# 130 constant matrix products of 26 forms ahead of the first real product of a two-layer encoder kernel

## The chip, the cores and the metric

The kernel runs on one core of a Trainium2 chip. The metric is the device time of one execution in microseconds. Two timed executions of the kernel before took 1747.62 and 1748.41 us; their median is 1748.01 us. A further execution was taken with the profiler, and every row quoted below is of that one; its span, from the first to the last instruction, is 1746.7 us.

The engines are named as the profile names them: PE is the matrix engine, PEld its loading of weights (which can run beside a product), DVE the vector engine, ACT the activation engine, POOL the general engine, SP the engine that issues most transfers. A product takes a block of weights of 128 rows and up to 128 columns, and a moving operand of 128 rows and up to 512 columns, and writes into one of eight banks of PSUM, the accumulation memory. All other tiles lie in SBUF, the on-chip memory, 128 partitions wide.

## The reference

Two layers of a speech encoder on 512 tokens of width 1024, in float32:

```python
for l in range(DEPTH):                                  # 2
    x = x + 0.5 * swiglu(rms_norm(x, ffn1_norm[l]), ffn1_w_gate[l], ffn1_w_up[l], ffn1_w_down[l])
    h = rms_norm(x, mix_norm[l])
    p = h @ w_in[l]
    attn = mla_group(p[..., :o_kv], p[..., o_kv:o_pe], p[..., o_pe:o_cv], ...)
    conv = conv_group(p[..., o_cv:], conv_w[l], conv_b[l], conv_ln_g[l], conv_ln_b[l])
    x = x + jnp.concatenate([attn, conv], axis=-1) @ w_out[l]
    x = x + 0.5 * swiglu(rms_norm(x, ffn2_norm[l]), ffn2_w_gate[l], ffn2_w_up[l], ffn2_w_down[l])
    x = rms_norm(x, post_norm[l])
```

`swiglu(x, g, u, d)` is `(silu(x @ g) * (x @ u)) @ d`, with an inner width of 2816. `mla_group` is chunk-causal attention with 8 heads on low-rank projections, `conv_group` a gated causal convolution of 31 taps with a layer norm.

## The kernel before

Everything is held with features on the partitions and the 512 tokens along the tile. To reach float32 accuracy, both operands of a large product are split into a high and a low part of type float32r, and each product of 128 features is three products on PE, in `mm3`: high by high (L209), high by low (L210), low by high (L211). Weights come from memory as float32 into tiles `raw` or `fr`, ACT copies out the high part (L157 in `load_w`, L299 in `split_into`), and DVE subtracts to get the low part (L164, L301). Both parts lie in one long tile, `weights`, used as a ring of four places for each part; a place can be filled again only when PE has used it. In most of the feed-forward work the moving operand has 256 columns (`HS`), elsewhere 512 (`S`).

Tiles for split activations and other passing data come from a pool named `ring` with 35 buffers (`slot()`, shown as `r` in the profile); each holds 512 float32, 2 KB in a partition. Banks of PSUM come from `bank()`, of which there are seven (`ps`).

The program is unrolled. Its text gives the order of priority; within that, and within the edges written by hand (`issue_after`, `in_turn`), a planner sets each engine's order of instructions and the places of the tiles by its own simulation of the program (`schedule_with_timeline_sim=True`). On the chip each engine then works through its list in order and waits on semaphores.

The opening, which the change touches, runs as follows. The first transfers are issued: one 4 KB row of gains by ACT (L129), the first piece of x by SP (L130). DVE fills `ones` with 1.0 (L133). PE then does ten float32 products of `ones` by `ones` into a bank that nobody reads (`awake`, L135 to L137; `WAKE` is 10); a float32 product is recorded as two passes, so there are 20 records. DVE fills further constants (L139 to L147). Meanwhile the pieces of x land, ACT and DVE split each into two parts (L222, L223), and ACT and DVE split the first weights, in halves of 512 columns (L1143, L1144). The first real products, each 512 columns wide, start as soon as the first piece of x and the first half of weights are there (L209 to L211, called from `plain_first`). While they go on, the sums of squares for the first norm are gathered (L239 to L246), and PE forms the norm's sums between the products of the first feed-forward block (L253); from these comes R, which scales every operand that follows (L389 and on).

Of the kernel before, what the change touches and what calls it, by code (L numbers as in the profile page):

```python
# [7 lines left out]
FP = mybir.dt.float32  # L8
FR = mybir.dt.float32r
BF = mybir.dt.bfloat16  # L10
# [5 lines left out]
P = 128  # L16
D = 1024
S = 512
# [19 lines left out]
HS = S // 2  # L38
# [45 lines left out]
def encoder_kernel(ctx: ExitStack, tc: tile.TileContext, xT, consts, vecs, rgain, wgu1, wd1, wdq1, wdr1,  # L84
# [11 lines left out]
    def nm(s):  # L96
        uid[0] += 1
        return f"{s}{uid[0]}"

    def slot(dt=FP, w=S):  # L100
        return ring.tile([P, w], dt, tag="r", name=nm("r"))
# [4 lines left out]
    def bank():  # L106
        return psum.tile([P, S], FP, tag="ps", name=nm("ps"))
# [14 lines left out]
    V, A, G, T = nc.vector, nc.scalar, nc.gpsimd, nc.tensor  # L122
# [12 lines left out]
    awake = bank()  # L135
    for _ in range(WAKE):
        T.matmul(awake[:, 0:P], ones, ones, start=True, stop=True)  # L137
    minus_half = cpool.tile([P, H], FP, name="minus_half")
    V.memset(minus_half, -0.5)  # L139
    onesm = cpool.tile([P, P], FP, name="onesm")  # L140
# [1191 lines left out]
```

## Time and profile before

| | before |
|---|---|
| median of two timed runs | 1748.01 us |
| the runs | 1747.62 to 1748.41 us |
| span of the profiled execution | 1746.7 us |
| PE busy | 1728.1 us, 12486 products |
| DVE busy | 1471.0 us |
| ACT busy | 1097.3 us |
| POOL busy | 388.7 us |
| moved by DMA | 231.56 MB, 133 GB/s on average |

Times in a row are starts from the beginning of the span, then durations. A row of the timeline may merge several instructions that follow each other (`x2`), and ends with the idle time before it and what ended that. The duration that the profile gives a product is its whole passage through the array, and products overlap: how fast they follow each other is read from their starts or from a count over a stretch, not from their durations. A record of a product is missing here and there.

### The profile page before, as it was taken

How to read it: one execution, taken by the hardware profiler on the slowest of the kernel's cores; microseconds unless marked ns; L12 is line 12 of the kernel's file. 1: busy time of each engine (PE TensorE's matmuls, PEld its weight loads, DVE VectorE, ACT ScalarE, POOL GpSimd, SP SyncE). 2: the span in 40 equal slices, each digit the busy share in tenths (PEclk: the TensorE clock that was granted, in tenths of full speed). 3: DMA queues.
4: the chain of work that ended last, by engine and by line, in shares of the span. 5: the costliest groups of instructions: out<-in, count | busy, mean ns of one | idle time of the engine just before them, and what ended most of it. 6: DMA issues, size and time to landing. Idle time of an engine off the chain costs nothing. (4 is left out here: it accounts for less than half of the span.)

```text
span 1746.7 us, 31482 instructions
## 1 busy us (share of the span) xinstructions
PE 1728.1 (99%) x12486; PEld 1579.1 (90%) x12486; DVE 1471.0 (84%) x2104; ACT 1097.3 (63%) x1711; POOL 388.7 (22%) x322
## 2 busy tenths in 40 slices
PE   9999999999999999999999999999999999999998
PEld 7899999888678899999889999997976788999997
DVE  7888888888965989897679989888989668888887
ACT  5576766567953476756645757665778435767665
POOL 1001000348823001000310010013676410010000
PEclk9999999999999999999999999999999999999999
DMA  5567575424303467675425575754251125675753
GB/s 184 144 155 185 142 197 112 136 88 118 80 25 102 116 160 177 159 172 138 124 72 163 131 202 133 196 121 130 83 148 35 56 83 145 155 184 143 191 117 101
DMA packets 76851, 231.56 MB, mean 133 GB/s; under 512 B 8736, under 2 KB 12960, under 8 KB 76704
## 3 DMA queue, kind: packets, MB, share of 16 engines
q1 hardware_dynamic: 58704, 171.87, 30.8%
q0 software_dynamic: 17856, 57.68, 19.3%
q8 instruction: 98, 1.61, 0.4%
q14 instruction: 49, 0.40, 0.1%
q10 hardware_dynamic: 144, 0.00, 0.0%
HBM read 225.33 MB, written 2.10 MB: 130 GB/s over the span
## 5 line engine op out<-in xcount | busy, mean ns | idle before, releaser
L210 PE MATMUL ps<-r,weights 128*128 128x256 f32 (+1 forms) x2620 | 810.2, 309 | 2.8 <-DVE r L223 2.8
L209 PE MATMUL ps<-r,weights 128*128 128x256 f32 (+1 forms) x2620 | 807.3, 311 | 0.8 <-ACT weights L1143 0.6
L211 PE MATMUL ps<-r,weights 128*128 128x256 f32 (+1 forms) x2380 | 741.2, 313 | 5.9 <-DVE weights L301 3.9
L210 PEld LDWEIGHTS ps<-r,weights 128*128 128x128 f32 x2620 | 492.0, 188 | 35.3 <-DVE r L223 4.1
L209 PEld LDWEIGHTS ps<-r,weights 128*128 128x128 f32 x2620 | 491.9, 188 | 33.9 <-issue 2.0
L211 PEld LDWEIGHTS ps<-r,weights 128*128 128x128 f32 x2380 | 446.8, 188 | 38.9 <-DVE weights L301 5.4
L209 PE MATMUL ps<-xj,weights 128*128 128x256 f32 x864 | 238.5, 276 | 0.0
L210 PE MATMUL ps<-xj,weights 128*128 128x256 f32 x864 | 238.5, 276 | 0.0
L299 ACT CAST weights<-fr 128x1024 fp32r<-128x1024 f32 (+2 forms) x178 | 168.4, 946 | 96.2 <-DVE fr L453 40.1
L157 ACT CAST weights<-raw 128x1024 fp32r<-128x1024 f32 (+4 forms) x124 | 112.1, 917 | 177.7 <-PE ps L210 114.0
L301 DVE TENSOR_TENSOR weights<-fr,weights 128x1024 fp32r<-128x1024 f32 (+2 forms) x178 | 195.1, 1096 | 31.4 <-ACT weights L299 31.3
L433 POOL DMA_DIRECT2D ls<-in_wgu x72 | 62.5, 868 | 703.1 <-ACT ls L432 619.9
L164 DVE TENSOR_TENSOR weights<-raw,weights 128x1024 fp32r<-128x1024 f32 (+4 forms) x108 | 119.8, 1118 | 64.1 <-ACT weights L157 63.4
L210 PEld LDWEIGHTS ps<-xj,weights 128*128 128x128 f32 x864 | 162.2, 188 | 0.0
L209 PEld LDWEIGHTS ps<-xj,weights 128*128 128x128 f32 x864 | 162.2, 188 | 0.0
L211 PE MATMUL ps<-xj,ls 128*128 128x256 f32 x576 | 159.0, 276 | 0.0
L301 DVE TENSOR_TENSOR weights<-raw,weights 128x1024 fp32r<-128x1024 f32 (+2 forms) x112 | 122.0, 1089 | 14.1 <-ACT weights L299 13.9
L299 ACT CAST weights<-raw 128x1024 fp32r<-128x1024 f32 (+2 forms) x112 | 105.2, 939 | 42.9 <-DVE raw L532 23.5
L1005 POOL TENSOR_TENSOR y<-y,pr 128x495 f32<-128x495 f32 (+29 forms) x90 | 119.3, 1328 | 45.8 <-ACT pr L1003 40.5
L432 ACT ACTIVATE ls<-fr 128x1024 fp32r<-128x1024 f32 (+2 forms) x62 | 59.9, 967 | 97.9 <-PE ps L211 64.2
L516 DVE SCALAR_TENSOR_TENSOR x<-ps,x 128x512 f32<-128x512 f32 x154 | 105.7, 686 | 8.6 <-PE ps L211 7.9
L211 PEld LDWEIGHTS ps<-xj,ls 128*128 128x128 f32 x576 | 108.1, 188 | 0.0
(260 smaller groups left out, 3013.9 us busy)
## 6 DMA issues: line engine op xcount, KB each, us to landing
fr<-in_wgu SPq DMA_DIRECT2D x112, 512.0 KB, 4.6
ls<-in_wgu POOLq DMA_DIRECT2D x72, 512.0 KB, 7.2
raw<-in_wgu SPq DMA_DIRECT2D x62, 512.0 KB, 5.3
fr<-in_wdq SPq DMA_DIRECT2D x48, 384.0 KB, 4.4
ls<-in_wdq POOLq DMA_DIRECT2D x32, 384.0 KB, 6.4
raw<-in_wd SPq DMA_DIRECT2D x32, 256.0 KB, 2.8
raw<-in_wcv SPq DMA_DIRECT2D x16, 512.0 KB, 3.5
raw<-in_wout SPq DMA_DIRECT2D x16, 512.0 KB, 3.4
```

Source lines behind the costliest of these rows:

```text
L157: order["cast"] = in_turn("h", lambda: A.copy(hi[:, :w], raw[:, :w]))
L164: in_turn(e, lambda: e.tensor_tensor(lo[:, :w], raw[:, :w], hi[:, :w].bitcast(FP), ALU.subtract))
L209: T.matmul(o, lh, rh, start=first, stop=False, skip_group_check=free)
L210: T.matmul(o, lh, rl, start=False, stop=False, skip_group_check=free)
L211: order["mm"] = T.matmul(o, ll, rh, start=False, stop=last, skip_group_check=free).ins
L299: in_turn("h", lambda: A.copy(hi[:, :w], src[:, :w]))
L301: order["lo"] = in_turn(V, lambda: V.tensor_tensor(lo[:, :w], src[:, :w], hi[:, :w].bitcast(FP), ALU.subtract))
L432: A.activation(lo[:, :n], src[:, :n], AF.Copy, scale=-1.0)
L433: G.dma_start(out=lo[:, :n], in_=w, accum_op=ALU.add)
L516: return V.scalar_tensor_tensor(v, o.rearrange("p (m t) -> p m t", m=2), 0.5 * sign, v, ALU.mult, ALU.add).ins
L1005: order["conv"] = G.tensor_tensor(ys[c][:, s:], ys[c][:, s:], pr[:, s:], ALU.add).ins
```

## The change

Directly behind the ten products of `ones` in the program's text, three slots of the ring are taken and filled by DVE: `pm` and `pw` of type float32r, 512 columns each, and `pb` of type bfloat16, 512 columns. Then PE does 26 groups of five equal products into the bank `awake`, 130 products in all. Nothing reads their result. The five of a group have the same weights and the same moving operand; the groups differ in these:

- 8 groups with 512 moving columns and 8 with 256, in which the weights start 0, 16, ... 112 elements into `pw`;
- 4 groups with 256 moving columns, weights starting 4, 8, 24 and 192 elements into `pw`;
- 256 moving columns that are all one column of `pm`, read with step zero; and 128 weights that are all one column of `pw`, with 256 moving columns;
- bfloat16 weights and moving operand, 256 and 512 columns;
- weights of 64 columns, with 256 and with 512 moving columns.

```diff
     awake = bank()
     for _ in range(WAKE):
         T.matmul(awake[:, 0:P], ones, ones, start=True, stop=True)
+    pm, pw = slot(FR), slot(FR)
+    pb = slot(BF)
+    V.memset(pm.bitcast(FP), 1.0)
+    V.memset(pw.bitcast(FP), 1.0)
+    V.memset(pb, 1.0)
+    forms = [(pw[:, 16 * j:16 * j + P], pm[:, 0:n]) for n in (S, HS) for j in range(8)]
+    forms += [(pw[:, j:j + P], pm[:, 0:HS]) for j in (4, 8, 24, 192)]
+    forms += [(pw[:, 0:P], pm[:, 0:1].to_broadcast([P, HS])), (pw[:, 16:17].to_broadcast([P, P]), pm[:, 0:HS]),
+              (pb[:, 0:P], pb[:, 0:HS]), (pb[:, 0:P], pb[:, 0:S]), (pw[:, 0:64], pm[:, 0:HS]), (pw[:, 0:64], pm)]
+    for w_, m_ in forms:
+        for _ in range(5):
+            T.matmul(awake[0:w_.shape[1], 0:m_.shape[1]], w_, m_, start=True, stop=True)
     minus_half = cpool.tile([P, H], FP, name="minus_half")
     V.memset(minus_half, -0.5)
```

## The prediction

> **What bounds the kernel now.** I read the page first: its span, the busy times and the costliest groups.
>
> ```profile
> span 1746.7 us, 31482 instructions
> ...
> PE 1728.1 (99%) x12486; PEld 1579.1 (90%) x12486; DVE 1471.0 (84%) x2104; ACT 1097.3 (63%) x1711; POOL 388.7 (22%) x322
> ...
> L210 PEld LDWEIGHTS ps<-r,weights 128*128 128x128 f32 x2620 | 492.0, 188 | 35.3 <-DVE r L223 4.1
> ```
>
> PE is busy for 99% of the span, so only 18.6 us of 1746.7 are without a product. A share of busy time alone would not show that PE is at its pace, so I read second the table by stretches.
>
> ```profile
> 30.00:50.00 20.00, 20.00 (x88) 16.23 (x87) 19.70 (x31) 8.94 (x15) 0.00 (x0) 1.00 0.22 65
> 50.00:100.00 50.00, 48.99 (x322) 43.84 (x322) 42.70 (x60) 30.04 (x43) 3.67 (x4) 1.00 0.60 159
> ...
> 300.00:400.00 100.00, 97.34 (x593) 87.60 (x592) 88.17 (x127) 60.68 (x113) 42.87 (x33) 1.00 0.36 102
> 400.00:500.00 100.00, 98.72 (x664) 71.53 (x663) 89.82 (x176) 74.30 (x160) 66.75 (x50) 1.00 0.31 84
> ...
> 1300.00:1400.00 100.00, 99.29 (x649) 70.39 (x648) 78.74 (x131) 69.78 (x150) 56.76 (x40) 1.00 0.22 62
> ...
> 1600.00:1700.00 100.00, 100.00 (x883) 99.92 (x883) 88.48 (x120) 66.43 (x93) 9.52 (x11) 1.00 0.63 155
> ```
>
> The columns after the length are busy time and count of PE, PEld, DVE, ACT and POOL, then PE's granted clock, the share of the DMA engines and GB/s. The last row is the feed-forward work at its pace: 883 products of 256 columns in 100 us, 113.3 ns each, at granted clock 1.00. A weight load takes 188 ns there (the row above) and still a product starts every 113 ns, so loads run beside products. DVE is busy for 88% of it and DMA for 63%: neither sets the pace. PE does, and work added to PE's list is paid for unless it falls where PE waits.
>
> So the third view is the timeline of the opening, where the change lies: PE's rows from the last products of `ones` on.
>
> ```profile
> 4.21 1.05 PE L137 MATMUL ps<-ones 128*128 128x128 f32 x6
> 5.07 0.50 PE L209 MATMUL ps<-r,weights 128*128 128x512 f32 x1
> 5.41 0.44 PE L210 MATMUL ps<-r,weights 128*128 128x512 f32 x1
> 6.46 0.50 PE L209 MATMUL ps<-r,weights 128*128 128x512 f32 x1 [0.60 <-ACT weights L1143]
> 6.79 0.40 PE L210 MATMUL ps<-r,weights 128*128 128x512 f32 x1
> 7.03 0.66 PE L211 MATMUL ps<-r,weights 128*128 128x512 f32 x2
> 7.54 0.72 PE L209 MATMUL ps<-r,weights 128*128 128x512 f32 x2
> 8.32 0.50 PE L210 MATMUL ps<-r,weights 128*128 128x512 f32 x1
> 8.66 0.40 PE L211 MATMUL ps<-r,weights 128*128 128x512 f32 x1
> 8.90 0.39 PE L210 MATMUL ps<-r,weights 128*128 128x512 f32 x1
> 9.13 0.40 PE L211 MATMUL ps<-r,weights 128*128 128x512 f32 x1
> 9.36 0.62 PE L209 MATMUL ps<-r,weights 128*128 128x512 f32 x2
> 9.82 0.39 PE L210 MATMUL ps<-r,weights 128*128 128x512 f32 x1
> ```
>
> The first real product starts at 5.07 us, right behind the products of `ones`. Until about 9.4 us the starts are uneven, because data arrives late; from then on they are even. The pace of 512 columns comes from the groups in the stretch 10 to 24.7 us and its last row of L210:
>
> ```profile
> L210 PE MATMUL ps<-r,weights 128*128 128x512 f32 x23 | 8.9, 389 | 0.0
> L211 PE MATMUL ps<-r,weights 128*128 128x512 f32 x22 | 8.2, 389 | 0.0
> L209 PE MATMUL ps<-r,weights 128*128 128x512 f32 x21 | 7.4, 389 | 0.0
> ...
> 24.55 0.39 PE L210 MATMUL ps<-r,weights 128*128 128x512 f32 x1
> ```
>
> These are 66 products, the first the one at 9.82 (it reaches past 10), the last the one at 24.55: 65 steps in 14.73 us, 226.6 ns each, twice the 113.3 ns of 256 columns.
>
> **The change, part by part.** *The products.* 512 columns move in 8 groups of the first kind, one of bfloat16 and one with 64 weight columns: 10 groups, 50 products. 256 columns move in 8 + 4 + 2 (the two broadcasts) + 1 + 1 = 16 groups, 80 products. By the paces above: 50 x 0.2266 + 80 x 0.1133 = 11.33 + 9.06 = 20.4 us. All are ahead of the real products in the program, and no operand of theirs comes from a transfer, so I put them on PE from 5.07 us to 25.5 us without a gap.
>
> The trace shows no bfloat16 product of this size, no broadcast operand, and no weights at these offsets under one moving tile. From above, the nearest row is a float32 product at L272, two passes of 512 columns; from below, products of 32 weight columns at L705, which share the array in strips:
>
> ```profile
> 30.81 1.02 PE L272 MATMUL ps<-t,ones 128*128 128x512 f32 x2
> ...
> 31.89 0.40 PE L210 MATMUL ps<-r,weights 128*128 128x512 f32 x1
> ...
> 445.96 3.60 PE L705 MATMUL ps<-r,m 128*32 128x512 f32 x32
> ```
>
> The two passes of L272 and one product of L209 lie between 30.81 and 31.89: (1.08 - 0.23) / 2 = 0.425 us a pass, 1.9 times 0.2266. If every form went at that, the products would cost 38.3 us. L705 does 32 products in 3.60 us, 0.113 us each, half of 0.2266; if the bfloat16 and the 64-column forms (20 products, 3.4 us of the sum) went at that, the sum would be 18.7 us. I take 20.4, because 110 of the 130 are float32r products of full weights, which is what L209 to L211 are.
>
> Here the Trainium skill has a lower price: the page "TensorE: Matmul & The Clock Gate", section "Back-to-back issue gap", states N / 2.4 + 2.5 ns, 215.8 ns for 512 columns and 109.2 for 256, by which the sum would be 19.5 us and the time 0.9 us lower. The trace has 226.6 and 113.3 at granted clock 1.00, so it does not agree, and the measured paces are used.
>
> *The fills.* DVE gets three fills of 512 elements ahead of its other constants.
>
> ```profile
> 0.84 0.17 DVE L133 MEMSET ones<- 128x128 f32 x1 [0.84 <-PEq L1324]
> ...
> 1.38 0.11 DVE L147 MEMSET mneg<- 1x64 bf16 x1
> 4.54 0.75 DVE L223 SCALAR_TENSOR_TENSOR r<-x,first_gain,r 128x512 fp32r<-128x512 f32 x1 [3.05 <-ACT r L222]
> ```
>
> 128 float32 take 0.17 us, so 512 take at most four times that, 0.68; three fills take at most 2.0 us. DVE is then done with its constants at about 3.5 us, and its next work starts at 4.54 after 3.05 us of idling. I cost the fills at nothing; if that idling were gone they would delay the first split by up to 2.0 us, which again would lie under the new products. `pm` and `pw` are filled by about 2.4 us, long before PE is through with `ones` at 5.07. No transfer is added, and SP's, ACT's and POOL's lists are untouched.
>
> *The stalls that go.* From 5.07 to 9.82 PE started 14 products (the rows above), which at the even pace need 14 x 0.2266 = 3.17 us; 4.75 passed. With the first real product at 25.5 us those 1.58 us of waiting should go, since what they waited for is done by then:
>
> ```profile
> 9.56 1.35 DVE L1144 TENSOR_TENSOR weights<-raw,weights 128x512 fp32r<-128x512 f32 x2
> 10.99 2.79 DVE L223 SCALAR_TENSOR_TENSOR r<-x,first_gain,r 128x512 fp32r<-128x512 f32 x4
> ```
>
> The first weights are split by 10.91 us and all of x by 13.78. Nothing is late next up to the norm's sums, because PE had no gap from 9.4 to 25.7 us before.
>
> *Later waits.* ACT, DVE and SP get 18.8 us ahead of PE in the opening, but cannot keep it: the four places of the `weights` ring come free only by PE, and R comes from PE's sums. After R, DVE is the late one (19.70 of 20 us busy in the row 30 to 50), and PE's next wait ends on it:
>
> ```profile
> 65.91 0.50 PE L211 MATMUL ps<-r,weights 128*128 128x512 f32 x1 [0.91 <-DVE weights L164]
> ```
>
> That work cannot start before R, so I let this wait stand and move with the rest (if it went, 0.9 us less). The three slots leave 32 of 35 in the ring until 25.5 us; the opening needs 16 for x and one for the squares, so no tile waits for them. They are free again when the operands after R are made.
>
> *Sum.* +20.4 - 1.6 = +18.8 us. The span of the profiled execution would be 1746.7 + 18.8 = 1765.5 us. The median of the timed runs stands 1.3 us above that span, and from it the time is 1748.0 + 18.8 = 1766.8 us, 1.1% more.
>
> **The rivals.** *A load is not hidden behind a product that uses the same weights.* This is the one that would make it slower by over 2%. Each group repeats one block of weights, and the stream of the trace changes blocks at nearly every product. If a load of 188 ns stood ahead of each new product, the sum would be 20.4 + 130 x 0.188 = 44.8 us and the time 1748.0 + 44.8 - 1.6 = 1791.2 us. It decides from a mean cost of 281 ns a product on, since 2% is 35.0 us and 35.0 + 1.6 over 130 is 0.281 (I have 0.157). For it: nothing in the trace repeats float32r weights. Against it: the products of `ones` do repeat theirs, and their loads run beside them,
>
> ```profile
> 4.22 0.85 PEld L137 LDWEIGHTS ps<-ones 128*128 128x128 f32 x5
> ```
>
> five loads in 0.85 us, less than 5 x 0.188, and the products in step with them. I give it 3 in 100. The Trainium skill has a sentence on its side: the page "TensorE: Matmul & The Clock Gate", section "The mechanism", has loads overlap products in flight only when their row groups differ, and here all 128 rows are used by each. The trace speaks against it: 188 ns loads over all 128 rows under products 113.3 ns apart.
>
> *Some offsets clash.* Weights and moving operand are both read from SBUF, and a bad distance might slow a read. If the 100 products of the 20 offset groups (40 x 0.2266 + 60 x 0.1133 = 15.9 us of the sum) took from a tenth to nine tenths more (the latter being L272's pace), the time would be 1768 to 1781 us. Against it: the same 113.3 ns holds over 100 us in which tiles from all over the ring meet weights at many places. For it: the weights there start at few distinct offsets. I give 9 in 100 to a clash that adds more than 2 us.
>
> *The planner orders the rest anew.* With 20 us more on PE its simulation may place tiles and order instructions differently far behind the opening. What it can win or lose is PE's waiting in the stretches that depend on order: 1.0 + 2.7 + 1.3 + 0.7 = 5.7 us in the rows 50 to 100, 300 to 500 and 1300 to 1400 above. All of it gone, or doubled, gives 1761 to 1772.5 us. Against it: most edges around the products are written out by hand. I give a shift of more than 2 us 13 in 100.
>
> *The products cost nothing.* That the time does not grow needs PE to have 18.8 us of later waits to give; outside the opening the whole span has less than 18.6. One in 100, the same for a planner's gain beyond that.
>
> **How the numbers follow.** The main case, 74 in 100, is 1766.8 us, by itself 1765 to 1769 (from 18.7 us of products to 2 us more than the sum). With the planner's ends and the lower half of the clash the range is 1761 to 1775; outside it I leave the upper clash, the unhidden loads and the no-cost case, about one in 10. The measurement tells about 2%, 35 us, from no change. Slower by over 2%: the unhidden loads and nothing else, 0.03. Faster by over 2%: no case gives it; 0.01 for what I do not see. Within 2%: 0.96.
>
> **What would show it.** In the profile after: 130 more products ahead of the first L209; the bfloat16 groups apart from the others in pace; the first L209 near 25.5 us, with even starts from there; PE busy near 1748 us; the wait that ends on L164 still there, 19 us later. A first L209 after 28 us means a clash or unhidden loads, to be read from the starts within each group. A first L209 near 25.5 us with a span outside 1764 to 1768 means that something behind the opening was reordered.

## The result and the profile after

The changed kernel took 1767.93 and 1769.65 us in two runs, a median of 1768.79 us against 1748.01 us: a ratio of 1.0113, 95% interval 1.0097 to 1.0130, or 20.8 us more (17 to 23 us by the interval). That is within the forecast range of 1761 to 1775 us and 2.0 us above the forecast of 1766.8 us. Against the 2% that was set as the measure, it counts as no change. The span of the profiled execution grew from 1746.7 to 1766.2 us, by 19.5 us. The trace after is that of the execution timed at 1767.93 us, 1.7 us above its span. The span before stands as far below the timed 1748.41 us, so that trace is most likely of this timed execution and not of a further one; the medians differ by more than the spans because the other two executions lie further apart.

The page of the kernel after, its first lines (busy time, share of the span and count of each engine):

```profile
span 1766.2 us, 31747 instructions
...
PE 1749.2 (99%) x12615; PEld 1598.6 (91%) x12616; DVE 1472.5 (83%) x2107; ACT 1099.1 (62%) x1711; POOL 388.3 (22%) x322
```

PE has 129 records more (one of the 130 is missing) and is busy for 21.1 us more; the other engines are busy as before. The timeline of PE in the opening of the kernel after, in rows that merge equal products; lines of the code are 12 higher behind the insertion, so that L221 is the old L209:

```profile
1.06 4.64 PE L137 MATMUL ps<-ones 128*128 128x128 f32 x20 [1.06 <-DVE ones L133]
5.35 18.25 PE L149 MATMUL ps<-r,r 128*128 128x512 f32 x110
23.44 1.80 PE L149 MATMUL ps<-r 128*128 128x256 bf16 x9
24.89 2.08 PE L149 MATMUL ps<-r,r 128*64 128x256 f32 x10
26.81 0.39 PE L221 MATMUL ps<-r,weights 128*128 128x512 f32 x1
27.04 0.40 PE L222 MATMUL ps<-r,weights 128*128 128x512 f32 x1
...
85.89 0.50 PE L223 MATMUL ps<-r,weights 128*128 128x512 f32 x1 [0.91 <-DVE weights L176]
```

The products stand where they were put, without a gap, and the first real product starts at 26.81 us instead of 5.07. From there the starts are even, 0.23 us apart: the stalls of the old opening are gone. The wait on the low part of the weights (old L164, now L176) is still there and as long as before, 0.91 us, at 85.89 instead of 65.91 us.

Setting each real product of one trace beside the same product of the other shows where the 20 us lie. It can be done for all, since both have 12486 records of products outside the new line, in nearly the same order:

```
start before, us        5.07    6.46    9.36   58.42    96.2 to 1536   1549 to 1707   1740.71 (last)
later by, us           21.74   20.81   20.18   20.09   19.9 to 20.3           19.4             20.01
```

All of it comes in the opening. In the following 1480 us it stays between 19.9 and 20.3 us. At 1549 us one wait of the trace before is not in the one after; the run with the fills alone, below, lacks it too, so it is not the products that took it away.

### The profile page after: what moved, and what is told of

It is laid out like the page before. It is cut to its first block, busy times and chain, and to the rows that moved or that the text cites. A ratio compares the mean times of both kernels' runs of the same rounds, so it can differ in the third digit from the quotient of the medians.

```text
span 1766.2 us, 31747 instructions
## 1 busy us (share of the span) xinstructions
PE 1749.2 (99%) x12615; PEld 1598.6 (91%) x12616; DVE 1472.5 (83%) x2107; ACT 1099.1 (62%) x1711; POOL 388.3 (22%) x322
## 4 chain that ended last, share of the span: by engine, by line
PE 68%; DVE 7%; ACT 2%; issue 1%; DMA 1%; SPq 0%; DVEq 0%; ACTq 0%
PE ps L223 21%; PE ps L221 21%; PE ps L222 21%; DVE cv L1011 1%; DVE mx L919 1%; PE ps L960 1%; PE ps L938 1%; DVE x L528 0%; ACT weights L311 0%; DVE x L646 0%; PE ps L717 0%; DVE r L941 0%; DVE weights L176 0%; DMA r<-m 0%; PE ps L265 0%
## 5 line engine op out<-in xcount | busy, mean ns | idle before, releaser
L221 PE MATMUL ps<-r,weights 128*128 128x256 f32 (+1 forms) x2620 | 808.0, 311 | 0.1
L221 PEld LDWEIGHTS ps<-r,weights 128*128 128x128 f32 x2620 | 491.9, 188 | 32.8 <-issue 2.0
L221 PE MATMUL ps<-xj,weights 128*128 128x256 f32 x864 | 238.5, 276 | 0.0
L176 DVE TENSOR_TENSOR weights<-raw,weights 128x1024 fp32r<-128x1024 f32 (+4 forms) x108 | 120.9, 1128 | 77.7 <-ACT weights L169 76.9
L221 PEld LDWEIGHTS ps<-xj,weights 128*128 128x128 f32 x864 | 162.2, 188 | 0.0
```

Of the source, the lines that this page charges most:

```text
L176: in_turn(e, lambda: e.tensor_tensor(lo[:, :w], raw[:, :w], hi[:, :w].bitcast(FP), ALU.subtract))
L221: T.matmul(o, lh, rh, start=first, stop=False, skip_group_check=free)
```

## The experiments

Times are compared with runs of the kernel before on the same chip. The runs without an interval had one timed execution and were made for their trace.

**The fills alone.** The three slots and the three fills stay, the 130 products are left out.

```diff
-    for w_, m_ in forms:
-        for _ in range(5):
-            T.matmul(awake[0:w_.shape[1], 0:m_.shape[1]], w_, m_, start=True, stop=True)
```

> The three fills of DVE and the three slots stay, the 130 products are left out. Theory (the products are the whole cost): DVE has about 3 us of idling for 1.4 us of fills, so the first real product starts at 5.07 us as before, PE's order behind it is the same, and the time is 1748 us within 1.5. Rival (fills, slots or the new places of tiles carry part of the 20.8 us): the first real product later than 5.5 us, or a time of 1750 us and more.

Measured: 0.9999 of the kernel before, interval 0.9990 to 1.0008, 1749.25 us. DVE's timeline of that run:

```profile
1.06 0.48 DVE L140 MEMSET r<- 128x512 f32 x1
1.60 0.48 DVE L141 MEMSET r<- 128x512 f32 x1
2.14 0.48 DVE L142 MEMSET r<- 128x512 bf16 x1
...
4.46 0.75 DVE L232 SCALAR_TENSOR_TENSOR r<-x,first_gain,r 128x512 fp32r<-128x512 f32 x1 [1.35 <-ACT r L231]
```

The fills take 1.5 us of DVE's idling, and 1.35 us of it are left before the first split. The first real product starts at 5.13 us. Fills and slots cost nothing here that the interval (1.7 us less to 1.4 us more) would show: the products are the whole cost.

**Ten of each.**

```diff
-        for _ in range(5):
+        for _ in range(10):
```

> Ten products a group instead of five, 260 in all. Theory (price per product plus a fixed part from the clock's rise): the second 130 run at full clock and cost what the groups of five show once the clock is up, 20.9 us, so the first real product starts 20.9 us later, at 47 to 48 us, and the time is 1789.7 us. In the trace only products that start before the clock's rise are slow. Rival (the 1.3 us over the sum are a fixed cost of starting such products, whatever the clock): slow products at the head again although the clock is up. Rival (loads of a repeated block are not hidden from some length of a group on): products 6 to 10 of a group slower than 2 to 5.

Measured: 1788.5 us, ratio 1.0223, interval 1.0207 to 1.0238; 38.8 us over the kernel before. The timeline of PE in that run:

```profile
5.35 35.78 PE L149 MATMUL ps<-r,r 128*128 128x512 f32 x220
40.98 3.42 PE L149 MATMUL ps<-r 128*128 128x256 bf16 x19
44.05 3.79 PE L149 MATMUL ps<-r,r 128*64 128x256 f32 x20
47.68 0.39 PE L221 MATMUL ps<-r,weights 128*128 128x512 f32 x1
```

The first real product starts 47.68 - 26.81 = 20.87 us later than with five of each: that is the price of 130 products once the clock is up. Only the first three are slow: their steps to the next start are 0.57, 0.43 and 0.39 us, and 0.24 or less in the float32r groups that follow. In the groups with offsets (the first left out) products 6 to 10 take 230 ns on average with 512 columns and 118 with 256, products 2 to 5 took 233 and 118; a load of 188 ns standing in the open would be far more, so no load of a repeated block does; the rival that would have made the change slower than 2% is out.

**The products in the middle of the feed-forward work.** The fills and products move from the opening to just before the fourth pair, behind PE's last product there, into a bank of their own. `constant_products` (not printed here) takes the bank and the three slots, fills them, does the 130 products of the change and returns the last.

```diff
+                    if l == 0 and w0 and p == 3:
+                        with tc.issue_after(order["pe"]):
+                            order["pe"] = constant_products()
                     act += pair(p, not last)
```

> The fills and the 130 products are moved from the opening to the fourth pair of the first feed-forward block, where PE has no waits; they write a bank of their own. Theory (PE's list is the bound, place matters only for waits and clock): the opening is that of before, first real product at 5.07 us; no cold clock; from the first of the 130 to the first real product behind them 20.9 us; nothing recovered; time 1748.0 + 20.9 = 1768.9 us. Rival (the later engines catch up): part of the 20.9 us comes back within 50 us because ACT, DVE and the transfers get ahead, time below 1767 us. Rival (the extra bank and slots make PE wait): over 1771 us.

Measured: 1782.17 us, ratio 1.0186, interval 1.0169 to 1.0203: 32.5 us more, where 20.9 was expected. The time is on the side of the second rival (over 1771 us), and PE did wait, but for the fills and not for a bank or a slot; that cause was in no theory. PE's timeline and the table by stretches (columns as in the prediction) show why:

```profile
104.81 3.75 PE L317 MATMUL ps<-r,r 128*128 128x512 f32 x8 [9.86 <-DVE r L309]
```

```profile
98.20:104.80 6.60, 0.00 (x0) 0.00 (x0) 6.19 (x11) 1.37 (x3) 0.00 (x0) 0.50 0.25 81
104.90:108.30 3.40, 3.40 (x8) 2.72 (x9) 0.40 (x1) 0.00 (x0) 0.00 (x0) 0.50 0.00 0
108.50:112.00 3.50, 3.50 (x17) 2.86 (x16) 0.00 (x0) 0.00 (x0) 0.00 (x0) 1.00 0.00 0
```

DVE works through its list in order and is the late engine in this stretch: the fills came at the end of a full list, and PE waited 9.86 us for them. During that wait PE's granted clock (the third number from the end) went to 0.50, and the first eight products behind it took 3.75 us where the full pace gives 7 x 0.227 + 0.39 = 1.98: 1.8 us more. 9.9 + 20.9 + 1.8 = 32.6 us, and between the real products on both sides the delay against the trace before jumps by 32.6 us. What was free in the opening cost 11.7 us here, since DVE had no idle time for it and PE had to wait until DVE's list came to the fills.

**The same with the fills one pair earlier.** This tells that reading apart from a disturbance by the bank and the slots. The edit is shown against the run before; `constant_tiles` (not printed) takes and fills the three slots.

```diff
+                    if l == 0 and w0 and p == 2:
+                        tiles = constant_tiles()
                     if l == 0 and w0 and p == 3:
                         with tc.issue_after(order["pe"]):
-                            order["pe"] = constant_products()
+                            order["pe"] = constant_products(*tiles)
```

> As the run with the products at the fourth pair, but the three fills are put one pair earlier in DVE's work. Theory (of the 32.6 us there, 9.9 were PE waiting for the fills in DVE's full list, 20.9 the products, 1.8 PE at half clock after that wait): without the wait the products cost 20.9 us, PE's clock stays up, and at most the 1.4 us of the fills come on top, since DVE sets the pace at about 65 us; time 1768.9 to 1770.5 us. Rival (the products disturb the pairs around them, by the bank or the slots they hold): 1775 us and more although no wait for the fills is left.

Measured: 1771.28 us, ratio 1.0132, interval 1.0115 to 1.0149, 22.2 us more (20 to 26 by the interval), a little beyond the expected 1770.5 us. The products themselves run from 97.40 us to the next real one at 118.28, 20.88 us, as expected. In the trace a further 3.1 us are lost, at another place than the products:

```profile
67.10 0.50 PE L211 MATMUL ps<-r,weights 128*128 128x512 f32 x1 [2.42 <-DVE weights L164]
```

```profile
66.00:67.00 1.00, 0.00 (x0) 0.00 (x0) 1.00 (x3) 0.45 (x1) 0.00 (x0) 1.00 1.07 217
67.70:71.00 3.30, 3.30 (x9) 2.65 (x8) 2.29 (x3) 0.25 (x1) 0.87 (x1) 0.50 0.91 187
71.10:75.00 3.90, 3.90 (x19) 3.23 (x18) 3.60 (x5) 2.28 (x3) 0.00 (x0) 1.00 0.75 209
```

The fills now lie at 62.6 to 64.7 us, in the stretch in which DVE is full, and the wait for L164 grew from 0.91 to 2.42 us, by just the fills' 1.5 us. And this wait too cost more than its length: the granted clock was 0.50 from 67.6 to 71.0 us, 9 products in 3.30 us where the full clock does about 14. The theory gave the first 1.5 us and missed the second part, about 1.6 us. With the products the delay against the trace before is 23.7 us, and it stays so for the next 100 us; the 22.2 us between the medians agree with that within their interval. The rival is out: the pairs around the products are not disturbed.

**Without the products of ones.**

```diff
-WAKE = 10
+WAKE = 0
```

> The ten products of ones are left out (WAKE = 0), the 130 products stay and come first on PE. Theory (the clock rises 3.5 to 5.6 us after PE's first work whatever that is, and at half clock a product takes twice as long): the 130 start when the second fill is done, at about 2.2 us, are at half clock until 4.6 to 6.7 us, which costs 1.2 to 2.2 us, and the first real product starts at 24.3 to 25.3 us instead of 26.8; time 1766.5 us. Rival (the clock is at the full from the start and the slow first products are a start-up of that kind of product): the first real product at 23.1 us or before.

Measured: 1765.86 us, ratio 1.0101, interval 1.0086 to 1.0116. PE's timeline, from three narrow windows:

```profile
2.14 4.64 PE L149 MATMUL ps<-r,r 128*128 128x512 f32 x10 [2.14 <-DVE r L141]
...
6.58 2.68 PE L149 MATMUL ps<-r,r 128*128 128x512 f32 x10
...
25.34 0.39 PE L221 MATMUL ps<-r,weights 128*128 128x512 f32 x1
```

The first ten products take 0.44 us each (6.58 - 2.14, over 10), twice the later pace; the next ten need 0.25 ((2.68 - 0.39) / 9). The trace's record of the granted clock begins at 7.05 us, at 1.00; that the clock was at half until then is read from these paces. From 2.14 to 7.05 half of the time is lost, 2.45 us: 2.14 + 20.9 + 2.45 = 25.5, and the first real product came at 25.34. It came out just beyond the expected 25.3, because the rise was later than any seen before. The trace is of the slowest of the four executions (1768.84 us; the others took 1765.7 to 1766.0). The rival (a start-up of such products at full clock) wanted 23.1 us.

**The forms in turn.** One of each form, five times over, instead of five of each.

```diff
-    for w_, m_ in forms:
-        for _ in range(5):
+    for _ in range(5):
+        for w_, m_ in forms:
```

> The same 130 products, but the 26 forms one after the other, five times over, instead of five of each. The 256-column products of the change took 118 ns where the kernel's own take 113.3, and the 512-column ones 231 where the kernel's take 226.6, but 226.6 at an offset of 256 bytes. Theory A (what counts is how the load of the next weights lies to the moving operand being read, modulo 256 bytes): among the eight 512-column forms the one ahead of the offset of 256 bytes is the clean one (226.6), the others 231; the 256-column ones stay near 118. Theory B (a product's own offset counts): the one at 256 bytes itself is clean. Theory C (loading the same block again and again is what costs): all 512-column forms at 226.6 and the 256-column ones at 113.3 ns, the sum 19.9 us instead of 20.9.

Measured: 1769.68 us, and 21.0 us from the first of the 130 (4.97) to the first real product (25.99). The steps from start to start of the eight forms of 512 columns, in the second of the five rounds, by the offset of the weights:

```
offset of weights, bytes      0    64   128   192   256   320   384   448
step to the next start, ns  233   229   233   241   235   229   232   226
```

Theory C falls: changing the block each time makes nothing faster. Theory B falls: the one at 256 bytes takes 235. Theory A foretold 226.6 at 192 bytes, ahead of 256, and got 241; it is right only at the last, whose next load lies 0 bytes from the moving tile. None of the three is right; none asks how a product falls into step with the load beside it, which the next runs try. The execution has one more loss, far from the products: a wait of 1.86 us that ends at 365.24 us, with 3.4 us at granted clock 0.50 behind it.

**Thirty of each, and the kernel's own pattern.** The 26 groups are replaced by 300 products in groups of 30; the bfloat16 tile and its fill are left out.

```diff
-    for w_, m_ in forms:
-        for _ in range(5):
-            T.matmul(awake[0:w_.shape[1], 0:m_.shape[1]], w_, m_, start=True, stop=True)
+    for n in (S, HS):
+        for j in (0, 16, 32, 48):
+            for _ in range(30):
+                T.matmul(awake[:, 0:n], pw[:, j:j + P], pm[:, 0:n], start=True, stop=True)
+    for _ in range(10):
+        for j, m in ((16, 0), (16, HS), (48, 0)):
+            T.matmul(awake[:, 0:HS], pw[:, j:j + P], pm[:, m:m + HS], start=True, stop=True)
+    for i in range(30):
+        T.matmul(awake[:, 0:HS], pw[:, 16:16 + P], pm[:, 0:HS], start=i == 0, stop=i == 29)
```

> Instead of the 26 groups, 300 products of float32r in groups of 30: 512 columns at offsets of 0, 64, 128 and 192 bytes, 256 columns at the same four; then 30 of 256 columns in the kernel's own pattern (weights at 64, 64, 192 bytes, moving halves 1, 2, 1), then 30 of 256 columns at 64 bytes that accumulate as the kernel's do. Theory (load of weights and moving operand collide by their distance modulo 256 bytes, after the first few of a group have fallen into step): settled 512 columns at 226.6 ns for offset 0 and 230 to 234 for the others, settled 256 columns at 113.3 for offset 64 and 117 to 121 for the others, the pattern and the accumulating ones at 113.3 to 114. Rival (distance counts for nothing once settled): all forms at 226.6 and 113.3. Rival (the kernel's pace needs its changing weights): the pattern alone at 113.3.

One row of PE's timeline for each group, each from a window inside it: 512 columns at 0, 64, 128, 192 bytes; 256 columns at the same four; the pattern; the accumulating ones.

```profile
7.73 4.70 PE L144 MATMUL ps<-r,r 128*128 128x512 f32 x20
12.73 6.70 PE L144 MATMUL ps<-r,r 128*128 128x512 f32 x28
19.72 6.67 PE L144 MATMUL ps<-r,r 128*128 128x512 f32 x28
26.68 6.57 PE L144 MATMUL ps<-r,r 128*128 128x512 f32 x28
33.43 3.52 PE L144 MATMUL ps<-r,r 128*128 128x256 f32 x28
37.03 3.34 PE L144 MATMUL ps<-r,r 128*128 128x256 f32 x27
40.57 3.49 PE L144 MATMUL ps<-r,r 128*128 128x256 f32 x28
44.13 3.34 PE L144 MATMUL ps<-r,r 128*128 128x256 f32 x27
48.24 2.66 PE L147 MATMUL ps<-r,r 128*128 128x256 f32 x22
51.07 3.11 PE L149 MATMUL ps<-r,r 128*128 128x256 f32 x26
```

A merged row reaches from the first start to the last end, so the pace is its length less one product (0.39 us for 512 columns, 0.28 for 256), over the count less one. That gives 227, 234, 233 and 229 ns for 512 columns; 120, 118, 119 and 118 ns for 256; 113 for the pattern and 113 for the accumulating ones. For 512 columns the theory holds: an offset of 0 is the clean one. For 256 it does not: 64 bytes, where the kernel's own products run at 113.3, stays at 118 when a block is repeated plainly behind a group at 0 bytes. In all these runs the moving tile starts at the same address modulo 256, by the addresses of the built program. So they do not tell the distance between the two operands from the address of the weights alone; where the text says distance, that choice is not shown. There is a hint for it in the trace before: products of 288 columns (L209 to L211, their moving operand in the `weights` ring), whose weights all start at one address modulo 256, follow each other at 131.6 ns on average at a distance of 0 (120 products) and at 133.3 ns at 128 bytes (72 products).

**The same with data.** Both tiles are filled with the first piece of x by ACT.

```diff
-    V.memset(pm.bitcast(FP), 1.0)
-    V.memset(pw.bitcast(FP), 1.0)
+    A.copy(pm, x[:, 0, :])
+    A.copy(pw, x[:, 0, :])
```

> As the run before, but both tiles are filled by ACT with the first piece of x instead of ones. Theory (addresses, not values, set the pace): the same pace in each group, within 1 ns of the run with ones. Rival (values count, by the power they draw or by the clock granted): paces slower than with ones by several per cent, or a lower granted clock in that stretch.

The rows of 512 columns at 0 and 64 bytes, of 256 columns at 0 bytes and of the pattern:

```profile
7.71 4.70 PE L144 MATMUL ps<-r,r 128*128 128x512 f32 x20
12.70 6.70 PE L144 MATMUL ps<-r,r 128*128 128x512 f32 x28
...
33.53 3.40 PE L144 MATMUL ps<-r,r 128*128 128x256 f32 x27
...
48.33 2.54 PE L147 MATMUL ps<-r,r 128*128 128x256 f32 x21
```

227, 234, 120 and 113 ns, as with ones: these two fillings, equal ones and the first piece of x, run alike.

**Which products stand ahead.** Nine groups of 30, all of 256 columns, in an order that separates two readings of the last two groups. They stand in place of the ten groups; the two tiles are filled with ones again.

```diff
+    pattern = ((16, 0), (16, HS), (48, 0))
+    for pairs, joined in ((pattern, 0), (((16, 0),), 0), (((0, 0),), 0), (((16, 0),), 1), (pattern, 0), (((48, 0),), 0),
+                          (((0, 0),), 0), (((0, 0), (0, HS)), 0), (((16, 0), (16, HS)), 0)):
+        for i in range(30):
+            j, m = pairs[i % len(pairs)]
+            T.matmul(awake[:, 0:HS], pw[:, j:j + P], pm[:, m:m + HS], start=not joined or i == 0,
+                     stop=not joined or i == 29)
```

> Nine groups of 30 products of float32r, 256 columns: the kernel's pattern; 64 bytes plain; 0 bytes plain; 64 bytes accumulating; the pattern; 192 bytes plain; 0 bytes plain; 0 bytes with the two moving halves in turn; 64 bytes with the two halves in turn. In the run before, 64 bytes plain stayed at 118 ns behind a group of 0 bytes, and 64 bytes accumulating stayed at 113.3 behind the pattern. Theory S (at 64 bytes there are two steady steps of load and product, and the products ahead decide which one holds): 64 plain behind the pattern at 113.3, 64 accumulating behind 0 bytes at 118. Theory T (accumulating products are the faster ones): 64 plain at 118 wherever it stands, 64 accumulating at 113.3 wherever it stands. Both: 0 bytes at 120. For 192 bytes S says 113.3 behind the pattern if that offset has the same two steps, 118 otherwise.

The second, third, fourth and sixth group (64 bytes plain behind the pattern; 0 bytes; 64 bytes accumulating behind 0 bytes; 192 bytes behind the pattern):

```profile
9.65 3.34 PE L146 MATMUL ps<-r,r 128*128 128x256 f32 x28
13.06 3.52 PE L146 MATMUL ps<-r,r 128*128 128x256 f32 x28
16.66 3.46 PE L146 MATMUL ps<-r,r 128*128 128x256 f32 x28
...
23.71 3.22 PE L146 MATMUL ps<-r,r 128*128 128x256 f32 x27
```

113.3, 120.0, 117.8 and 113.1 ns. Theory S holds in each: at 64 and at 192 bytes there are two steady steps, 113 and 118, and the products ahead decide which one holds, whether a product accumulates or not. The kernel's pattern of three gets into the fast one by itself, within four products behind a group of accumulating ones; 0 bytes is at 120 behind anything tried. Taking the two moving halves in turn changes nothing: the last two groups are at 120.0 ns (0 bytes) and 117.8 (64 bytes).

The offset of the group ahead does not foretell the step alone. In the run with ten of each, the plain group at 64 bytes stands behind ten products at 0 bytes and takes the fast step; the one at 320 bytes, which is 64 modulo 256, stands behind ten at 256, which is 0, and takes the slow one:

```profile
25.86 0.96 PE L149 MATMUL ps<-r,r 128*128 128x256 f32 x7
...
30.42 0.99 PE L149 MATMUL ps<-r,r 128*128 128x256 f32 x7
```

These are 113 and 118 ns. What in the products ahead decides was not found.

## Why the prediction was right, point by point

*PE is the bound, and work added to its list is paid for.* Right. The first real product came 21.74 us later, the last 20.01 us later, and no stage behind the opening moved by more than 0.7 us. With 260 products the next 130 cost 20.87 us more at the first real product, and 38.8 - 20.8 = 18.0 us more in the medians, each set against the kernel before of its own session; the two intervals, each some 3 us to either side, do not tell this from 20.87.

*The fills cost nothing.* Right in the opening, and the run with the fills alone shows it. The reason given (3.05 us of DVE's idling) is what decides: in the two other places fills of the same 1.5 us cost 11.7 us and about 3 us, where DVE was full.

*The stalls that go: 1.58 us.* Right. The delay falls from 21.74 us at the first real product to 20.18 at 9.4 us, by 1.56, and to 20.09 at 58 us, by 1.65 in all.

*Later waits stay.* Right: the wait for the low part of the weights is 0.91 us in both.

*The products: 20.4 us from 5.07 to 25.5.* Mis-sized by 1.3 us; the first real product behind them started at 26.81. Two parts make this up. The first is the clock, which the sum did not have at all. The row of the products of `ones` in PE's timeline of the kernel before shows how far it goes:

```profile
1.06 4.20 PE L137 MATMUL ps<-ones 128*128 128x128 f32 x20 [1.06 <-DVE ones L133]
```

That is the kernel before; the same 20 passes took 4.64 us after, with the first start at 1.06 in both. The trace's record of the granted clock begins with the full clock, at 4.64 us before and at 6.44 after; that it rose there from half is read from the paces. So the last passes of `ones` stayed slow, and the first new product started at 5.35 instead of 5.07. The three that follow took 6.63 - 5.35 = 1.28 us where the pace gives 0.68:

```profile
5.35 1.44 PE L149 MATMUL ps<-r,r 128*128 128x512 f32 x3
...
6.63 0.40 PE L149 MATMUL ps<-r,r 128*128 128x512 f32 x1
```

Together 0.28 + 0.60 = 0.88 us, half of the 1.8 us by which the rise came later, which is what half pace loses. The rise was not made later by the change: over the runs in which PE starts at 1.06 us it lay between 4.57 and 6.74 us, at 4.57 in the run with the forms in turn, which has the same work on PE up to there. Where real products stand right behind those of `ones`, a late rise cost nothing that can be seen, since PE waits for data then: in the run with the products midway the rise came at 6.00 us, and the real products at 10 us stood 0.6 us earlier than in the kernel before.

The second part is the pace. Leaving out those three, 127 products took 20.18 us; at 226.6 and 113.3 ns they would have taken 47 x 0.2266 + 80 x 0.1133 = 19.71. The 0.47 us are the clash of offsets (some 0.07 us more, by which the bfloat16 products were quicker, are taken off it), which was a rival with 9 in 100 for more than 2 us. It exists, but it is small, 1 to 6% of a product and not a tenth and more. The rows of the kernel after for 512 and 256 columns:

```profile
6.86 8.25 PE L149 MATMUL ps<-r,r 128*128 128x512 f32 x35
...
15.41 6.81 PE L149 MATMUL ps<-r,r 128*128 128x256 f32 x56
```

These are (8.25 - 0.39) / 34 = 231 ns and (6.81 - 0.28) / 55 = 119 ns on average. The argument against this rival, that the kernel's even 113.3 ns holds at "many places", was wrong: by the addresses of the built program, of the kernel's products with weights from the `weights` ring, all of 512 columns have weights at 0 bytes modulo 256 from the moving tile, and all but 24 of those of 256 columns at 64 or 192. The kernel's text shows it too: `WOFF = 16, 48` moves the high and the low part by 16 and 48 elements, 64 and 192 bytes. These are the offsets at which the fast step exists. The two bounds that the prediction took from L272 and L705 were both far off: the bfloat16 products took 110 and 215 to 216 ns, those of 64 columns 113 to 117 and 224 to 236, neither half of the full product's pace nor 1.9 times it.

*The lower price by the page "TensorE: Matmul & The Clock Gate" of the Trainium skill.* The section "Back-to-back issue gap" gives 109.2 and 215.8 ns by its formula, which it calls the gap of an isolated product; for a stream of loads and products it has about 131 ns for 512 columns, which no form here comes near. The bfloat16 products of the run with ten of each, 256 and 512 columns, run at the formula:

```profile
41.09 1.04 PE L149 MATMUL ps<-r 128*128 128x256 bf16 x8
...
42.29 1.67 PE L149 MATMUL ps<-r 128*128 128x512 bf16 x7
```

Less the length of one (0.27 and 0.38 us), (1.04 - 0.27) / 7 = 110 ns and (1.67 - 0.38) / 6 = 215 ns. So the formula of the Trainium skill agrees with the trace for bfloat16, and the float32r products are 4 to 5% above it at their best. Taking the measured pace for the sum was right.

*The loads are hidden.* Right. The sentence of the Trainium skill, page "TensorE: Matmul & The Clock Gate", section "The mechanism", that loads overlap only where row groups differ is not what these runs show, with the same block of 128 rows loaded 30 times at 113 ns a product; the other case of that section, a load into a background weight buffer, fits them.

*The planner.* Its new order made no difference that can be seen: the 12486 real products stand in the same order in the two traces but for 48 places in the opening.

The sum, term by term: 20.4 + 0.28 + 0.60 + 0.47 - 1.65 = 20.1 us, the delay found at 58 us and at the end. The medians differ by 20.8 us, which the interval of 17 to 23 us does not tell from 20.1.

So the mechanism was right, and the two terms that the sum put at nothing, the clock and the offsets, came to 1.35 us. That they stayed so small is in part luck: over the rises seen, from 4.57 to 6.74 us, the clock's share lies between nothing and about 1 us, and neither it nor a bound for it was worked out beforehand. The price of the offsets was bounded, and came out below the lower end of that rival.

## What to carry to other kernels

Work added to the list of the bounding engine costs its own time, and it can be priced to a few per cent from the starts of its like; what remains is the state that it meets, here the clock of the first microseconds. A small fill or copy is free only where its engine is idle: look at the list that it joins, since 1.5 us on an engine that was late were paid for twice here, as the wait and as the slower clock behind the wait. A pace that is even over a whole kernel says nothing on other addresses if the kernel's addresses all stand at the same distances.

## What the runs showed of the hardware

- The granted clock of PE fell after short waits. A wait of 1.86 us (forms in turn) and one of 2.42 us (fills one pair earlier) were each followed by 3.4 us at 0.50. In the wait of 9.86 us (midway) the clock fell 3.2 us after its start and stayed at 0.50 for 10.24 us, the last 3.6 of them with work.
- In each trace the changes of the clock lie whole multiples of 3.413 us apart. On that grid, from the rise on and leaving aside the last 15 us of each trace, 0.50 followed each of the five stretches in which PE had no product for 54% of the time or more, and none of those with 51% or less. The two cases nearest to each other are the forms in turn, with PE busy for 1.55 of 3.41 us, and the run with data, with 1.66 of 3.41 after a wait of 1.75 us; each has the following stretch below it, PE's clock third from the end:

```profile
362.97:366.38 3.41, 1.55 (x7) 0.95 (x6) 3.41 (x4) 0.00 (x0) 1.67 (x1) 1.00 0.48 153
366.38:369.79 3.41, 3.41 (x10) 2.64 (x9) 0.74 (x2) 0.00 (x0) 0.00 (x0) 0.50 0.00 1
...
493.90:497.31 3.41, 1.66 (x19) 0.63 (x20) 2.87 (x4) 3.41 (x10) 3.18 (x4) 1.00 0.93 313
497.31:500.70 3.39, 3.39 (x30) 1.44 (x19) 0.58 (x2) 1.54 (x4) 1.80 (x2) 1.00 0.50 195
```

- The clock rose between 3.5 and 5.7 us after PE's first work, in eleven traces: ten whose first product came at 1.06 us (rise at 4.57 to 6.74), and one at 2.14 us (rise at 7.05). In each it rose at the end of the first stretch of that grid in which PE was busy throughout; stretches with PE busy for 64 and 66% (ten of each; which products stand ahead) did not raise it. As far as these traces show, the place of the grid against the first product sets how many products are slow.
- A product of float32r runs at 113.3 ns for 256 columns and 226.6 for 512 at best; at other distances between weights and moving operand modulo 256 bytes (or other addresses of the weights, which is not told apart) it takes 118 to 120 and 229 to 234. At 64 and 192 bytes a stream of 256 columns has two steady steps, and keeps the one that it came in with.
- With the moving operand read at step zero the five products of 256 columns took 111 ns each in the kernel after, where those at the same offset with a plain moving operand took 118 to 120 on average; why was not tried.
